# Split feed-forward weights: cut twice, or cut once, stored to DRAM and loaded again

## The chip, the cores and the metric

The kernel runs on one core of a Trainium2 chip. Its time is the device time of one execution in microseconds (us). The core has TensorE (PE, matrix products; its weight loads are shown apart as PEld), VectorE (DVE), ScalarE (ACT), GpSimd (POOL) and SyncE (SP), which here only issues DMAs. PEclk is the granted clock of TensorE as a share of full speed.

## What is computed

The reference chains two blocks over 2048 tokens of width 1024: a state-space and short convolution block, and then a block with a convolution module, a gated recurrence, chunked attention and a feed-forward part. Only the last part matters here, cut to its lines:

```
h = x * (1.0 + sc2) + sh2
gt, up = jnp.split(h @ w_ffn_in[l], 2, axis=-1)
y = (jax.nn.silu(gt) * up) @ w_ffn_out[l]
x = layer_norm(ALPHA * x + (1.0 + g2) * y, ln2_g[l], ln2_b[l])
```

All is float32. `w_ffn_in` is 1024 x 5632 (2816 gate columns, 2816 up columns), `w_ffn_out` 2816 x 1024. An operand of a product is scaled by a power of two and split into a high and a low f16 part; a product of two such operands is three f16 matmuls: high by high, high by low, low by high.

## The kernel before

The feed-forward part runs twice over the weights, once for each half of the tokens (1024). A half has two stages. The first makes the products with `w_ffn_in`, 256 columns at a time: a gate pair, then the up pair of the same columns, 11 of each, so 22 pairs for each half. The second makes the products with `w_ffn_out` and finishes rows (residual, layer norm); rows of the first half are finished while the second half's input products run.

The products of one pair use a scheme with 7 block products in place of 8 (`products`, L1967). Each block product is 4 slices of 128 by 3 f16 matmuls (lines L400, L401, L402), so 12 matmuls with 512 tokens; a pair has 84, a half 1848. Results leave PSUM by VectorE (L1979) and ScalarE (L1984).

A pair's weights (class `Pair`) go through three steps, in both halves alike:

- `load`: two DMAs of 512 KB (L1860) on SP's queue, into two raw float32 tiles.
- `scale`: two sums of squares on ScalarE (L393), their sum on VectorE (L1869), a reduction over all partitions on POOL (L361), a power of two from it on VectorE (L351 to L353).
- `cut`: four combinations of blocks on POOL (L357, 128x512 each), then four splits, each by one ScalarE instruction for the high part (L388) and one on VectorE for the low part (L389). The result is four f16 tiles of 7168 values per partition in all. Then the raw tiles are freed.

`Feed` decides when a pair's steps are issued: during the products of pair i (`ahead`, `later`) it issues the load, scale and cut of pair i+1 and the load and scale of pair i+2, as far as the arena (a planner of SBUF space) has room. A DMA that writes a raw tile waits until the cut of the pair that had the space before is done. SP issues its DMAs in the order in which they stand; one that waits holds up those behind it. All of the kernel's loads and stores named here stand in that one queue.

During the second half, SP also carries the loads and stores of the rows that are being finished (L2111 to L2135), which POOL and VectorE work on.

Of the kernel before, what the change touches and what calls it, by code (L numbers as in the profile page):

```python
# [10 lines left out]
F16 = mybir.dt.float16  # L11
# [9 lines left out]
P = 128  # L21
# [11 lines left out]
class Arena:  # L33
    def __init__(self, ap, n, unit, slack, small=0, zone=None):
        self.small = small
        self.zone = n if zone is None else zone
        self.ap = ap
        self.unit = unit
        self.slack = slack
        self.segs = [(0, n, 0)]  # L40
        self.now = 0
        self.live = {}
# [71 lines left out]
    def free(self, v):  # L114
        _, st, n, _ = self.live.pop(id(v))
        self.now += 1
        self.segs.append((st, st + n, self.now))
        self.segs.sort()
        old = self.now - self.slack
        out = []  # L120
        for s in self.segs:
            if out and out[-1][1] == s[0] and out[-1][2] <= old and s[2] <= old:
                out[-1] = (out[-1][0], s[1], max(out[-1][2], s[2]))
            else:
                out.append(s)
        self.segs = out
# [26 lines left out]
class Weight:  # L153
# [10 lines left out]
    def load(self):  # L164
        k = self.k
        self.raw = k.several([([P, self.nkb, P], F32, "raw")] * (self.ncol // P))
        for c, raw in enumerate(self.raw):
            k.nc.sync.dma_start(raw, self.src[:, c * P:(c + 1) * P].rearrange("(k p) c -> p k c", p=P))
# [101 lines left out]
class Kit:  # L270
# [69 lines left out]
    def keep(self, src):  # L340
        t = self.hold()
        self.nc.vector.tensor_copy(t, src)
        return t
# [755 lines left out]
def load_hT(k, dr_h, tb, t=None):  # L1099
    t = t or k.retry(lambda: k.pair([P, KB, TB], "hT"))  # L1100
    for x in range(2):
        k.nc.sync.dma_start(t[x].rearrange("p a b -> p (a b)"), dr_h[tb, x])
    return t
# [275 lines left out]
def stage_conv_att(k, ca, dr, hT, nxt):  # L1379
    att = None  # L1380
    for tb in range(NTB):
        if tb == 1:
            nxt()
        nh = None
        if tb + 1 < NTB:
            try:
                nh = k.pair([P, KB, TB], "hT") if AHEAD else None
            except MemoryError:
                pass
        if nh is not None:  # L1390
            load_hT(k, dr["h1"], tb + 1, nh)
        ca.proj(tb, hT)
        if nh is None and tb + 1 == NTB:
            nh = load_hT(k, dr["h1"], 0)
        k.free(*hT)
        hT = nh or load_hT(k, dr["h1"], tb + 1)
        if tb == 0:
            att = k.bg.add(ca.steps(), ATT_RATE)
            taps = k.bg.add(ca.taps(), EARLY_RATE)
    return att, taps, hT  # L1400
# [312 lines left out]
def stage_mix2(k, mx, dr, steps, taps, nxt):  # L1713
# [43 lines left out]
    def pairs(m):  # L1757
        he, ho = hs
        hs.clear()
        S, S_ = (k.new([P, 2, 512], F32, "S") for _ in range(2))  # L1760
        a11, a12, a21, a22 = he[:, :512], he[:, 512:], ho[:, :512], ho[:, 512:]
        k.gtt(S[:, 0], a21, a22, ALU.add)
        k.gtt(S[:, 1], S[:, 0], a11, ALU.subtract)
        k.gtt(S_[:, 0], a11, a21, ALU.subtract)
        k.gtt(S_[:, 1], a12, S[:, 1], ALU.subtract)
        later.append(lambda: cut(m, he, ho, a22, S, S_))
# [82 lines left out]
    return mv, k.rsqrt(mv[:, 1:2], 1.0, 1e-5)  # L1849


class Pair:
    def __init__(self, k, src, xinv):
        self.k, self.src, self.xinv = k, src, xinv

    def load(self):
        k = self.k
# [4 lines left out]
    def scale(self):  # L1862
        k = self.k
        ss = k.tiny("wss", 3)
        junk = k.new([P, 4, 2 * P], BF16, "junk")
        for i in range(2):
            k.sumsq(junk, self.raw[i], out=ss[:, i:i + 1])
        k.free(junk)
        k.nc.vector.tensor_tensor(ss[:, 2:3], ss[:, 0:1], ss[:, 1:2], ALU.add)  # L1869
        self.cols = k.cols3.pop(0) if len(k.cols3) > 8 else k.hold(3)  # L1870
        tot, self.s, self.inv = (self.cols[:, i:i + 1] for i in range(3))
        k.allsum(ss[:, 2:3], tot)
        k.pow2(tot, out=(self.s, self.inv))
        k.nc.vector.tensor_tensor(self.inv, self.inv, self.xinv, ALU.mult)

    def cut(self):
        k = self.k
        x, y = self.raw
        got = k.several([([P, 2, 4, 2 * P], F16, "w2")] * 2 + [([P, 2, 8, P], F16, "w3"), ([P, 2, 4, P], F16, "w1"), ([P, 8, P], F32, "T"), ([P, 4, P], F32, "T")])
        self.w, self.T = got[:4], got[4:]  # L1880
        b11, b12, b21, b22 = x[:, :, :P], x[:, :, P:], y[:, :, :P], y[:, :, P:]
        T, T4 = self.T
        T2, T3 = T[:, 0:4], T[:, 4:8]
        k.gtt(T3, b22, b12, ALU.subtract)
        k.gtt(b12, b12, b11, ALU.subtract)
        k.gtt(T2, b22, b12, ALU.subtract)
        k.gtt(T4, T2, b21, ALU.subtract)
        for i in (1, 0, 2, 3):
            t = self.w[i]
            k.split(t[:, 0], t[:, 1], (x, y, T, T4)[i], self.s)  # L1890
        k.free(*self.raw, *self.T)
        self.raw = self.T = None

    def block(self, b):
        t, o = ((self.w[0], 0), (self.w[1], 0), (self.w[1], P), (self.w[0], P), (self.w[2], 0), (self.w[2], 4), (self.w[3], 0))[b]
        if t.shape[3] == 2 * P:
            return [(t[:, 0, i, o:o + P], t[:, 1, i, o:o + P]) for i in range(4)]
        return [(t[:, 0, o + i], t[:, 1, o + i]) for i in range(4)]

    def free(self):  # L1900
        self.k.free(*self.w)
        self.k.cols3.append(self.cols)


class Feed:
# [30 lines left out]
class FFN:  # L1936
# [7 lines left out]
    def prep(self, inv_h, ln):  # L1944
        k, a = self.k, self.a
        self.ln = ln
        DFF = self.FB * P
        Wi = a["w_ffn_in_2"][0]
        self.chunks = [Feed([Pair(k, Wi[:, c + f * P:c + f * P + 2 * P], inv_h) for f in range(0, self.FB, 2) for c in (0, DFF)]) for _ in range(2)]

    def prime(self, hf):
        f = self.chunks[hf]
# [251 lines left out]
@with_exitstack  # L2204
def two_blocks(ctx, tc, a, out):
    k = Kit(ctx, tc)
    dp = ctx.enter_context(tc.tile_pool(name="dr", bufs=1, space=DRAM))
    dr = {
        "u": dp.tile([512, 8, 256], F32, name="u_d"),
        "y": dp.tile([512, 8, 256], F32, name="y_d"),  # L2210
        "yv": dp.tile([512, T], F32, name="yv_d"),
        "mod": dp.tile([1, 6 * D], F32, name="mod_d"),
        "x2": dp.tile([T, D], F32, name="x2_d"),
        "y2": dp.tile([T, D], F32, name="y2_d"),
        "x3": dp.tile([T, D], F32, name="x3_d"),
        "z": dp.tile([T, 512], F32, name="z_d"),
        "h1": dp.tile([NTB, 2, P, KB * TB], F16, name="h1_d"),
        "h2": dp.tile([4, 2, P, 28 * P], F16, name="h2_d"),
        "ext": dp.tile([4, P * 768 + 768], F32, name="ext_d"),
    }  # L2220
    xT, chunks, ssm, mod = stage_in(k, a, dr)
    ca = ConvAtt(k, a, dr)
    rec = Rec(k, a, dr)
    mx = Mix2(k, a, dr)
    ff = FFN(k, a, dr, out)
    tk = {}

    def start_c(tb, ih, hb):
        if tb == 1:
            tk["c"] = k.bg.add(ca.prep(ih, hb), 1.0)  # L2230
        if tb == 2:
            tk["hT"] = load_hT(k, dr["h1"], 0)

    inv_h, hb2 = stage_glu_mix(k, a, xT, chunks, ssm, mod, dr, start_c)
    k.bg.drain(tk["c"])

    def start_r():
        tk["r"] = k.bg.add(rec.prep(inv_h), 1.0)

    att, taps, hT = stage_conv_att(k, ca, dr, tk["hT"], start_r)  # L2240

    def start_m():
        tk["m"] = k.bg.add(mx.prep(), 0.4)

    steps = stage_rec(k, rec, dr, hT, att, taps, start_m)
    k.bg.drain(tk["m"])
    ff.prep(mx.inv_h, mx.ln)
    hT = stage_mix2(k, mx, dr, steps, taps, lambda t: ff.prime(0) if t >= PRIME_AT else None)
    ff.run(hT)
# [26 lines left out]
```

## Time and profile before

| | us |
|---|---|
| three runs | 3523.9, 3524.34, 3530.92 (median 3524.34) |
| profiled execution, span | 3526.9 |
| first half, input products | 2068 to 2536 |
| first half, output products | 2543 to 2777 |
| second half, input products | 2777 to 3280 |
| second half, output products | 3287 to 3510 |

The page gives the profiled execution's span and no other time of it, so sums are made against that span. The stages are read from the times of the matmuls by line. A row of groups shows: line, engine, operation, tiles written and read, count, busy time, mean ns, then the idle time of the engine before these instructions and what ended it. A row of windows shows for each engine its busy time in a stretch, the granted clock, the DMA engines' share and GB/s. A row of waits shows the engine and line, what released it, and then the total, the number and the longest.

### The profile page before, as it was taken

Reading aid. Unit: us, or ns where it says so; the run is one execution under the profiler, and the core shown is the slowest. Engines: PE = TensorE matmul, PEld = TensorE weight load, DVE = VectorE, ACT = ScalarE, POOL = GpSimd, SP = SyncE. Lnnn points to the kernel's source line nnn. Section 1 sums busy time; section 2 is a strip of 40 time slices with the busy share of each in tenths; the row PEclk is TensorE's granted clock in tenths of the full one; section 3 lists DMA queues with packets and bytes.
Section 4 is the critical chain, followed back from the end, with each engine's and each line's share of the span. In section 5 each row is a group of like instructions: output and inputs, shape, how many; then the busy total and the mean of one; then the engine's idle time right before and its main releaser. Section 6 shows DMA issues by size and latency. Waiting matters only on the chain. (4 is left out here: it accounts for less than half of the span.)

```text
span 3526.9 us, 44439 instructions
## 1 busy us (share of the span) xinstructions
PE 3094.7 (88%) x16116; PEld 1533.4 (43%) x16116; DVE 2270.6 (64%) x5218; ACT 1285.4 (36%) x1986; POOL 916.3 (26%) x1018
## 2 busy tenths in 40 slices
PE   5688999999689888999899968898799987997998
PEld 3244444534245554555554423343344432433444
DVE  5475877366655579997678776666523587655446
ACT  4322222574335564222243335554411233443210
POOL 0243335033332332010301233332101344321012
PEclk9889999999889999999999989999999998998999
DMA  8623534435475661100347972211414112111421
GB/s 181 145 74 86 134 89 105 109 102 161 140 237 108 120 140 37 37 33 16 105 132 166 242 203 90 96 54 46 139 58 144 62 63 79 45 48 48 152 90 51
DMA packets 534844, 367.79 MB, mean 104 GB/s; under 512 B 290952, under 2 KB 480328, under 8 KB 530528
## 3 DMA queue, kind: packets, MB, share of 16 engines
q1 hardware_dynamic: 534624, 364.95, 38.1%
q8 instruction: 126, 2.06, 0.2%
q14 instruction: 94, 0.77, 0.1%
HBM read 236.91 MB, written 67.66 MB: 86 GB/s over the span
## 5 line engine op out<-in xcount | busy, mean ns | idle before, releaser
L400 PE MATMUL psum<-arena 128*128 128x512 f16 (+2 forms) x4272 | 1617.1, 380 | 254.4 <-ACT arena L388 161.8
L402 PE MATMUL psum<-arena 128*128 128x512 f16 (+2 forms) x4272 | 1613.1, 379 | 33.5 <-DVE arena L389 30.1
L401 PE MATMUL psum<-arena 128*128 128x512 f16 (+2 forms) x4272 | 1616.0, 380 | 19.3 <-DMA arena<-h_d 15.4
L357 POOL TENSOR_TENSOR arena<-arena 128x64 f32<-128x64 f32 (+4 forms) x794 | 785.4, 1010 | 1617.8 <-issue 300.8
L400 PEld LDWEIGHTS <-arena 128*128 128x128 f16 x4272 | 428.4, 100 | 704.8 <-ACT arena L388 144.4
L389 DVE SCALAR_TENSOR_TENSOR arena<-arena,kept 128x1024 f16<-128x1024 f32 (+2 forms) x394 | 480.6, 1244 | 334.0 <-ACT arena L388 332.6
L388 ACT ACTIVATE arena<-arena,kept 128x1024 f16<-128x1024 f32 (+2 forms) x394 | 388.5, 1013 | 771.9 <-DVE kept L352 256.1
L402 PEld LDWEIGHTS <-arena 128*128 128x128 f16 x4272 | 427.0, 100 | 546.7 <-DVE arena L389 49.7
L401 PEld LDWEIGHTS <-arena 128*128 128x128 f16 x4272 | 427.0, 100 | 537.2 <-issue 100.4
L393 ACT ACTIVATE arena<-arena 128x1024 bf16<-128x1024 f32 (+2 forms) x262 | 284.0, 1084 | 492.2 <-DVE arena L2038 93.4
L361 POOL PARTITION_ALL_REDUCE kept<-ring x95 | 49.5, 529 | 614.0 <-issue 265.1
L1979 DVE TENSOR_TENSOR arena<-arena,psum 128x512 f32<-128x512 f32 x264 | 176.1, 679 | 24.1 <-PE psum L402 14.7
L351 DVE TENSOR_SCALAR ring<-kept 128x1 int32<-128x1 int32 x141 | 20.7, 151 | 249.0 <-POOL kept L361 217.4
L1350 DVE SCALAR_TENSOR_TENSOR arena<-arena 128x512 f32<-128x512 f32 x240 | 177.7, 775 | 0.3
L1532 PE MATMUL psum<-arena 128*127 128x64 f32 (+6 forms) x896 | 103.6, 260 | 21.5 <-DVE arena L1535 20.7
L1532 PEld LDWEIGHTS psum<-arena 128*127 128x127 f32 (+6 forms) x896 | 99.6, 178 | 47.8 <-DVE arena L1535 29.0
L389 DVE SCALAR_TENSOR_TENSOR arena<-arena,ring 128x1024 f16<-128x1024 f32 x76 | 103.6, 1374 | 21.2 <-ACT arena L388 21.2
L388 ACT ACTIVATE arena<-arena,ring 128x1024 f16<-128x1024 f32 x76 | 85.9, 1141 | 82.2 <-DVE ring L352 44.8
L753 DVE SCALAR_TENSOR_TENSOR arena<-arena 128x128 f32<-128x128 f32 x336 | 105.0, 349 | 1.6
L1270 ACT ACTIVATE arena<-arena,ring,kept 128x640 f32<-128x640 f32 (+4 forms) x64 | 54.4, 851 | 91.0 <-DVE ring L1268 74.7
L2038 DVE SCALAR_TENSOR_TENSOR arena<-arena,kept 128x512 f32<-128x512 f32 x88 | 78.9, 898 | 1.2
L1534 DVE TENSOR_TENSOR arena<-arena 128x256 f32<-128x256 f32 x112 | 55.7, 497 | 34.2 <-PE psum L1532 33.5
(315 smaller groups left out, 2662.5 us busy)
## 6 DMA issues: line engine op xcount, KB each, us to landing
arena<-in_w_ffn_in_dram SPq DMA_DIRECT2D x88, 512.0 KB
arena<-in_w_in_dram SPq DMA_DIRECT2D x50, 512.0 KB
arena<-in_w_ada_dram SPq DMA_DIRECT2D x48, 512.0 KB
arena<-h_d SPq DMA_DIRECT2D x22, 1024.0 KB
arena<-in_w_ffn_out_dram SPq DMA_DIRECT2D x88, 256.0 KB
arena<-in_x_dram SPq DMA_DIRECT2D x32, 512.0 KB
x_d<-arena SPq DMA_DIRECT2D x32, 512.0 KB
arena<-in_w_ffn_out_dram SPq DMA_DIRECT2D x22, 512.0 KB
```

What stands on the lines that cost most here:

```text
L357: self.nc.gpsimd.tensor_tensor(out, x, y, op)
L388: self.nc.scalar.activation(hi, src, AF.Identity, scale=s)
L389: self.nc.vector.scalar_tensor_tensor(lo, src, s, hi, op0=ALU.mult, op1=ALU.subtract)
L393: self.nc.scalar.activation(junk, src, AF.Square, accum_out=ss)
L400: self.nc.tensor.matmul(ps, lh, rh, start=start and i == 0, stop=False)
L401: self.nc.tensor.matmul(ps, lh, rl, start=False, stop=False)
L402: self.nc.tensor.matmul(ps, ll, rh, start=False, stop=stop and i == n - 1)
L753: v.scalar_tensor_tensor(ac, raw[:, kb], cc[:, kb:kb + 1], ac, op0=ALU.mult, op1=ALU.add)
L1350: v.scalar_tensor_tensor(acc[:, f], src, w, acc[:, f], op0=ALU.mult, op1=ALU.add)
L1532: nc.tensor.matmul(pv[:rows, bsl], KS[:, c * P:c * P + rows], q4[:, bsl], start=True, stop=True)
L1979: v.tensor_tensor(out, x, ps, op)
L2038: v.scalar_tensor_tensor(g[f][:, j], u, wu.inv, g[f][:, j], op0=ALU.mult, op1=ALU.mult)
```

## The change

In the first half, the last act of `cut` now is `keep`: the four f16 tiles of a pair are stored to a DRAM array `w2` (22 pairs, 128 partitions, 7168 values), by four DMAs on SP's queue, three of 512 KB and one of 256 KB, 1.835 MB for each pair, 88 DMAs in all. In the second half a new class `Again` takes the place of `Pair`: its `load` is four DMAs from that array straight into four f16 tiles; its `scale` and `cut` do nothing, and the inverse scale is the one that the first half kept. In place of two raw loads of 512 KB each, a pair of the second half has those four.

```
+PIECES = ((0, (2, 4, 2 * P)), (2048, (2, 4, 2 * P)), (4096, (2, 8, P)), (6144, (2, 4, P)))
...
-        self.cols = k.cols3.pop(0) if len(k.cols3) > 8 else k.hold(3)
-        tot, self.s, self.inv = (self.cols[:, i:i + 1] for i in range(3))
+        tot, self.s, self.inv = k.tiny("ptot"), k.tiny("ps"), k.hold()
...
         for i in (1, 0, 2, 3):
             t = self.w[i]
             k.split(t[:, 0], t[:, 1], (x, y, T, T4)[i], self.s)
+        self.keep()
         k.free(*self.raw, *self.T)
...
+    def keep(self):
+        for (o, shape), t in zip(PIECES, self.w):
+            n = shape[0] * shape[1] * shape[2]
+            self.k.nc.sync.dma_start(self.kept[:, o:o + n], t.rearrange("p x a b -> p (x a b)"))
...
     def free(self):
         self.k.free(*self.w)
-        self.k.cols3.append(self.cols)
...
+class Again(Pair):
+    def __init__(self, first):
+        self.k, self.first, self.kept = first.k, first, first.kept
+
+    def load(self):
+        k = self.k
+        self.inv = self.first.inv
+        self.w = k.several([([P, *shape], F16, "w%d" % i) for i, (_, shape) in enumerate(PIECES)])
+        for (o, shape), t in zip(PIECES, self.w):
+            n = shape[0] * shape[1] * shape[2]
+            k.nc.sync.dma_start(t.rearrange("p x a b -> p (x a b)"), self.kept[:, o:o + n])
+
+    def scale(self):
+        pass
+
+    def cut(self):
+        pass
...
-        self.chunks = [Feed([Pair(k, Wi[:, c + f * P:c + f * P + 2 * P], inv_h) for f in range(0, self.FB, 2) for c in (0, DFF)]) for _ in range(2)]
+        cols = [c + f * P for f in range(0, self.FB, 2) for c in (0, DFF)]
+        first = [Pair(k, Wi[:, c:c + 2 * P], inv_h, self.dr["w2"][i]) for i, c in enumerate(cols)]
+        self.chunks = [Feed(first), Feed([Again(w) for w in first])]
...
+        "w2": dp.tile([FFN.FB, P, 7168], F16, name="w2_d"),
```

Lines move by the change: the raw load L1860 becomes L1863, the store is L1900, the new load L1922, and later lines stand 28 further (L2073 becomes L2101). On SP's queue, the end of the first half's input products and the start of the output products before (`in_w_ffn_in` are raw loads of weights, `in_w_ffn_out` those of the output products, `h_d` activations):

```order
L1860 DMA arena<-in_w_ffn_in_dram 128x4x256 x4
L2018 DMA arena<-in_w_ffn_out_dram 128x1024 x2
L1860 DMA arena<-in_w_ffn_in_dram 128x4x256 x16
L2073 DMA arena<-in_w_ffn_out_dram 128x512 x7
L2169 DMA arena<-h_d 128x4x1024
```

and the end of the same stretch now (`w_d` is the array `w2`):

```order
L1863 DMA arena<-in_w_ffn_in_dram 128x4x256 x2
L1900 DMA w_d<-arena 128x2048 x3
L1900 DMA w_d<-arena 128x1024
L1863 DMA arena<-in_w_ffn_in_dram 128x4x256 x2
L1900 DMA w_d<-arena 128x2048 x3
L1863 DMA arena<-in_w_ffn_in_dram 128x4x256
L1900 DMA w_d<-arena 128x1024
L1863 DMA arena<-in_w_ffn_in_dram 128x4x256
L2101 DMA arena<-in_w_ffn_out_dram 128x512 x4
L1900 DMA w_d<-arena 128x2048 x3
L1900 DMA w_d<-arena 128x1024
L1922 DMA arena<-w_d 128x2048
```

Between the loads of one pair and the next, four stores of the pair that has just been cut now stand; the last two loads L1863 apart are those of pair 21.

In the second half ScalarE before had, for each pair, squares (the L393 rows) and four cuts (the three and one L388 rows) between the PSUM copies L1984 and the activations' own squares and cuts (those with `ring`):

```order
L388 ACTIVATE arena<-arena,ring 128x1024 x2
L1984 COPY arena<-psum 128x512
L388 ACTIVATE arena<-arena,kept 128x1024 x3
L388 ACTIVATE arena<-arena,kept 128x512
L393 ACTIVATE arena,ring<-arena 128x1024 x2
L2029 ACTIVATE arena<-arena,kept 128x1024 x2
L1984 COPY arena<-psum 128x512
```

and now has only the copy and the activations' work:

```order
L2012 COPY arena<-psum 128x512
L393 ACTIVATE arena,kept<-arena 128x1024
L388 ACTIVATE arena<-arena,ring 128x1024
L393 ACTIVATE arena,kept<-arena 128x1024
L2012 COPY arena<-psum 128x512
L388 ACTIVATE arena<-arena,ring 128x1024
```

The weights' squares (L393 into `ring`) and cuts (L388 with `kept`) are gone from between the copies; what stays belongs to the activations and, as L2029 before and L2057 now, to the gate.

More of the change, by code (lines that the diff above doesn't have):

```diff
@@ L1849, in ln_stats, with __init__ @@
     return mv, k.rsqrt(mv[:, 1:2], 1.0, 1e-5)
+PIECES = ((0, (2, 4, 2 * P)), (2048, (2, 4, 2 * P)), (4096, (2, 8, P)), (6144, (2, 4, P)))
 class Pair:
-    def __init__(self, k, src, xinv):
-        self.k, self.src, self.xinv = k, src, xinv
+    def __init__(self, k, src, xinv, kept):
+        self.k, self.src, self.xinv, self.kept = k, src, xinv, kept
     def load(self):
```

## The prediction

> **What bounds the kernel now.** I read the page's first line, then cut the span at the stages of the feed-forward part, and then read TensorE's waits in each of them.
>
> ```profile
> PE 3094.7 (88%) x16116; PEld 1533.4 (43%) x16116; DVE 2270.6 (64%) x5218; ACT 1285.4 (36%) x1986; POOL 916.3 (26%) x1018
> core 0: us, PE busy (x) PEld busy (x) DVE busy (x) ACT busy (x) POOL busy (x), PEclk, DMA share, GB/s
> 2068.00:2536.00 468.00, 401.86 (x1765) 173.78 (x1764) 290.47 (x476) 230.36 (x313) 132.71 (x104) 0.94 0.29 89
> 2543.00:2777.00 234.00, 231.53 (x1057) 104.01 (x1057) 74.01 (x111) 45.51 (x64) 26.05 (x21) 0.99 0.31 104
> 2777.00:3280.00 503.00, 421.96 (x1849) 182.03 (x1848) 332.90 (x571) 200.03 (x261) 174.43 (x137) 0.93 0.19 64
> ```
>
> TensorE is the bound of the whole, and the rows are, in order: the input products of the first half of the tokens (all but some 80 matmuls; the records lack a few), the output products of that half, and the input products of the second half. Output products keep TensorE busy for 231.53 of 234 us. Input products don't: 81 us are missing in the second half and 66 in the first. The waits of TensorE say for what; first the second half, then the first:
>
> ```profile
> PE psum L400 <- ACT arena L388: 66.6, 10, 15.7
> PE psum L402 <- DVE arena L389: 14.2, 15, 1.7
> ...
> PE psum L400 <- ACT arena L388: 40.4, 11, 7.5
> PE psum L402 <- DVE arena L389: 13.3, 15, 1.8
> ```
>
> L388 and L389 make the f16 high and low part of a weight tile, so TensorE waits for weights to be cut. The chain ahead of a cut is seen on late pairs 20 and 21 of the first half (SP's queue, then POOL, ScalarE, TensorE):
>
> ```profile
> 2466.33 0.37 SPq L1860 DMA_DIRECT2D arena<-in_w_ffn_in_dram  x1
> 2469.22 0.37 SPq L1860 DMA_DIRECT2D arena<-in_w_ffn_in_dram  x1
> 2487.97 0.37 SPq L1860 DMA_DIRECT2D arena<-in_w_ffn_in_dram  x1
> 2491.63 0.37 SPq L1860 DMA_DIRECT2D arena<-in_w_ffn_in_dram  x1
> ...
> 2473.01 3.98 POOL L357 TENSOR_TENSOR arena<-arena 128x512 f32<-128x512 f32 x3 [3.82 <-DMA arena<-in_w_ffn_in_dram]
> 2482.82 0.40 POOL L361 PARTITION_ALL_REDUCE kept<-ring  x1 [5.83 <-issue]
> 2490.33 1.27 POOL L357 TENSOR_TENSOR arena<-arena 128x512 f32<-128x512 f32 x1 [7.10 <-issue]
> ...
> 2483.64 3.23 ACT L388 ACTIVATE arena<-arena,kept 128x1024 f16<-128x1024 f32 x3 [6.05 <-DVE kept L352]
> 2511.98 3.23 ACT L388 ACTIVATE arena<-arena,kept 128x1024 f16<-128x1024 f32 x3 [5.67 <-DVE kept L352]
> ...
> 2485.88 0.39 PE L400 MATMUL psum<-arena 128*128 128x512 f16 x1 [1.68 <-ACT arena L388]
> 2514.22 0.61 PE L400 MATMUL psum<-arena 128*128 128x512 f16 x1 [6.72 <-ACT arena L388]
> ```
>
> One raw buffer pair is left there, so the loads of pair 21 start only when pair 20 is cut (2487.97, 2491.63), land some 3.8 us later, and sums, all-reduce and cuts follow. TensorE starts pair 20 at 2485.88 and pair 21 at 2514.22, each as soon as its first cut is there.
>
> **Second half: what goes.** All of that chain is removed there for 22 pairs: 4 combinations and an all-reduce on POOL, 2 squares and 4 cuts on ScalarE, 4 cuts on VectorE and small scale work. In the groups of that stage:
>
> ```profile
> L357 POOL TENSOR_TENSOR arena<-arena 128x512 f32<-128x512 f32 x118 | 166.6, 1425 | 203.9 <-issue 78.8 <-DMA arena<-in_w_ffn_in_dram 59.1 <-ACT arena L393 15.2
> L361 POOL PARTITION_ALL_REDUCE kept<-ring x19 | 7.8, 414 | 112.1 <-issue 85.8 <-DVE arena L2113 13.8 <-DVE ring L1869 6.7
> L389 DVE SCALAR_TENSOR_TENSOR arena<-arena,kept 128x1024 f16<-128x1024 f32 x60 | 81.4, 1384 | 16.8 <-ACT arena L388 16.5
> L389 DVE SCALAR_TENSOR_TENSOR arena<-arena,kept 128x512 f16<-128x512 f32 x20 | 17.2, 859 | 18.5 <-ACT arena L388 18.5
> ```
>
> About 19 to 20 pairs are cut inside this stage (2 or 3 were primed during the output products, where TensorE is full). What is left for VectorE is at most 332.90 - 81.4 - 17.2 = 234 us, and less for ScalarE and POOL: none can bound a stage of 400 us.
>
> What TensorE gives then follows from its spacing, running free and just after a long stall:
>
> ```profile
> 2481.66 0.38 PE L401 MATMUL psum<-arena 128*128 128x512 f16 x1
> 2483.82 0.38 PE L402 MATMUL psum<-arena 128*128 128x512 f16 x1
> ...
> 2882.56 0.61 PE L400 MATMUL psum<-arena 128*128 128x512 f16 x1 [13.64 <-ACT arena L388]
> 2885.70 0.63 PE L400 MATMUL psum<-arena 128*128 128x512 f16 x1
> 2887.84 0.63 PE L402 MATMUL psum<-arena 128*128 128x512 f16 x1
> ```
>
> Between the first two rows lie 10 matmuls, so 2.16/10 = 0.216 us each; between the last two 5, so 2.14/5 = 0.428, half the rate. A pair is 84 matmuls (7 products of 12), 22 pairs are 1848, and at 0.2157 (the spacing with one more digit, over longer stretches) that is 398.6 us; at the mean of the output products (231.53/1057 = 0.219) it is 405. The stage takes 503. Its loss of 104 is 66.6 + 14.2 = 80.8 of stalls, and 503 - 80.8 - 398.6 = 23 of slow matmuls behind stalls, which go with them. [...]
>
> I keep 5 us for what remains (the rows' other waits, and the 405 above), from 1 to 15: the second half gains **99 us** (90 to 104).
>
> **Second half: what comes.** Four loads for each pair, 1.835 MB in place of 1.05 MB, 88 in all, on SP. At TensorE's pace of 18.1 us (84 x 0.2157) they need 1.835/18.1 = 101 GB/s. What the same queue moved in its best and in a common stretch:
>
> ```profile
> 2680.00:2690.00 10.00, 10.00 (x48) 4.54 (x47) 3.52 (x5) 1.15 (x2) 1.26 (x1) 1.00 0.89 282
> 1990.00:2000.00 10.00, 10.00 (x48) 4.54 (x47) 7.82 (x21) 4.60 (x5) 2.89 (x3) 1.00 1.03 211
> ```
>
> So 6.5 to 8.7 us of 18.1. The loads write their tiles as soon as an earlier pair's products have read them; by the order of waits that is at least 140 matmuls, or 30 us, before TensorE reads them. They share SP with the rows of the first half that are being finished:
>
> ```profile
> SPq L2135 <- POOL arena L357: 102.1, 16, 29.5
> ```
>
> Here SP waits for POOL up to 29.5 us, with loads behind it. POOL's long delays come from the weight work that leaves, so I cost this at 0, and at 1 to 3 waits of 15 us if it stays: 0 to 45 us, kept as a rival below.
>
> **First half: what is added.** 88 stores, 1.835 MB for each pair, 3 pieces of 512 KB and one of 256 KB, each behind its cut, in SP's queue. An issue takes 0.37 us of SP. For a late pair, three stores now stand ahead of the next pair's first load and a fourth ahead of its second. These loads are on the chain. The issue costs at least 3 x 0.37 = 1.1 us for the first load and 1.5 for the second; beyond it, up to 1.57 MB are begun ahead of the load's bytes, 5.6 us at 282 GB/s and 7.4 at 211, if nothing of it had drained. But the pieces are cut at least 3.23/3 = 1.1 us apart (row 2483.64), and a piece of 0.52 MB needs 1.9 us at 282: I estimate that about half has drained when the load is issued. So 1.1 to 7.4 us, and I take 3.5 for the pair. Two things point up: the second load decides when POOL starts (row 2473.01), and it stands behind the most. From the trace, the chain passes a delay to TensorE in full: in the late pairs TensorE waits at each start.
>
> How many pairs? Pairs 18 to 21 have a single raw buffer, so the load waits for the cut: 4 x 3.5 = 14 us. In the pairs before, a second raw buffer lets a load go ahead of the cut, by the order; I take 2 us for all of them. One early place is worse, where the weights of pair 3 are loaded:
>
> ```profile
> 2109.85 1.37 SPq L1860 DMA_DIRECT2D arena<-in_w_ffn_in_dram  x2
> 2115.99 6.18 POOL L357 TENSOR_TENSOR arena<-arena 128x512 f32<-128x512 f32 x4 [13.73 <-DMA arena<-in_w_ffn_in_dram]
> 2131.80 0.61 PE L400 MATMUL psum<-arena 128*128 128x512 f16 x1 [5.54 <-ACT arena L388]
> ```
>
> POOL had been idle for 13.73 us when those bytes came, and TensorE stood for 5.54 at the pair's start. Pair 2's four stores now precede this load: 1.79 MB, 6.3 us at 282 and 8.5 at 211, against 1.5 of issue alone. I take 7. Sum: 14 + 2 + 7 = **23 us** lost, from 8 (4 x 1.1 + 1.5 + 2) to 40 (4 x 7.4 + 8.5 + 2).
>
> [...]
>
> **Sum.** The profiled execution spans 3526.9 us, 2.6 above the median of 3524.34. 3526.9 - 99 + 23 = 3451; against the median 3524.3 - 76 = **3448 us**. Its own range, by the bounds, is 3524.3 - 104 + 8 = 3428 to 3524.3 - 90 + 40 = 3474.
>
> **The rivals.**
>
> *Stores cost nothing* in the first half: stores drain while ScalarE still cuts, and only the second half's 99 count: 3425. For it speaks that the first half moves 89 GB/s of 282 seen; against it the four late loads that wait for the very cuts that the stores follow.
>
> *More of the first half pays.* If the stores cost 4 us on each of the last 11 pairs, not 4, the loss is 44 + 7 = 51, so 3524 - 99 + 51 = 3476. For it: 11 waits of TensorE on L388 in that half, so most late pairs have no slack. Against: their loads were issued earlier.
>
> *The loads of the second half become the bound.* At the 89 GB/s of the first half as a whole, 1.835 MB take 20.6 us, 22 pairs 453 us: 50 gained, 23 lost, 3497. The same comes of three waits of SP on POOL of 15 us. Against: 282 GB/s seen, 30 us of lead.
>
> *Slower.* In the first half SP's queue becomes the bound: each store waits for its cut, and every next pair's load waits behind it for all of the 1.57 MB. At 5.6 us for each of 22 pairs that is 123 - 99 = 24 us more than before: 3548. It decides from 99/22 = 4.5 us a pair. For it: a load behind a store that waits for a cut can't be early any more. Against: early pairs have a spare raw buffer, and the order leaves loads ahead of stores there.
>
> *It doesn't do what it says*: TensorE could wait in the second half for activations instead (L388's other work, or the sums that empty PSUM), which the weight work now hides. VectorE's 234 us in 400 speak against it; 30 us of it would give 3478, inside the range.
>
> **How the numbers follow.** Forecast 0.58 (3448); stores free 0.13 (3425); more of the first half 0.16 (3476); loads or activations bound the second half 0.07 (3490); slower 0.06 (3548). The likeliest case's own range is 3428 to 3474; the range 8 times in 10 is 3426 to 3488. A measurement of this kernel tells 0.2%, 7 us, from no change. Faster 0.92, same 0.02, slower 0.06.
>
> **What would show it.** In the profile after, the second half's input products should take 398 to 410 us, with TensorE's waits on cut weights gone and PEclk near 0.99; a wait on the new loads there means the third rival. In the first half the stage should take 490, not 468; waits for L388 should grow in the last four pairs and at pair 3. If that stage grows by under 8, the stores are free; by over 40, more pairs pay. The output products should stay at 234 and 223 us. Wrong it is if SP's waits hold back loads in either half by more than the cover named.

## The result, and the profile after

The changed kernel takes 3444.64 us (median of 4 runs, 3438.11 to 3448.44) beside 3526.59 of the kernel before on the same occasion: a ratio of 0.977, with a 95% interval of 0.9755 to 0.9784, 82 us faster. Measured again later beside other kernels it took 3445.32 where the kernel before took 3534.07: 0.9749 (0.9735 to 0.9762), 89 us faster. The forecast was 3448, 76 faster, in a range of 3426 to 3488.

The windows of the changed kernel's stages, and below them its waits of TensorE in the first half's input products (the second half's list of waits is empty; the 16.5 us, in pair 1, stand in place of 11.6 there and 5.8 at the start of pair 2 before):

```profile
core 0: us, PE busy (x) PEld busy (x) DVE busy (x) ACT busy (x) POOL busy (x), PEclk, DMA share, GB/s
2068.00:2548.00 480.00, 408.37 (x1766) 175.42 (x1765) 289.54 (x476) 231.84 (x315) 134.01 (x104) 0.93 0.49 167
2555.00:2785.00 230.00, 229.85 (x1056) 103.56 (x1056) 61.92 (x88) 30.18 (x44) 12.92 (x10) 0.99 0.35 120
2785.00:3184.00 399.00, 399.00 (x1850) 180.72 (x1849) 204.37 (x393) 81.51 (x104) 49.61 (x38) 1.00 0.35 113
3195.00:3426.00 231.00, 230.73 (x1056) 103.74 (x1055) 113.22 (x211) 29.42 (x44) 29.85 (x22) 0.99 0.24 85
```

```profile
PE psum L400 <- ACT arena L388: 47.6, 13, 7.0
PE psum L400 <- ACT arena L2012: 16.5, 1, 16.5
PE psum L402 <- DVE arena L389: 7.3, 8, 1.8
```

In the second half TensorE now never stops: 399.00 us busy of 399.00, clock 1.00, all 22 pairs 18.1 us long. That is the floor worked out beforehand. In the first half the stage grew. To see where, the pairs were counted off in the matmul records, 84 matmuls to a pair. Lengths in us, each from one profiled execution; the rows below the change are the experiments that follow:

| | pairs 0-1 | pairs 2-9 | pairs 10-16 | pairs 17-21 | first half | second half |
|---|---|---|---|---|---|---|
| before | 73.5 | 179.4 | 136.8 | 113.2 | 502.9 | 502.8 |
| the change | 72.6 | 182.4 | 136.5 | 123.7 | 515.3 | 398.9 |
| the change, again | 71.0 | 184.9 | 138.3 | 123.9 | 518.1 | 398.9 |
| stores only | 71.2 | 185.6 | 138.7 | 124.9 | 520.4 | 505.5 |
| small stores | 72.2 | 176.5 | 136.0 | 116.0 | 500.7 | 506.4 |
| scale once, no stores | 71.6 | 175.7 | 135.9 | 113.8 | 496.9 | 425.9 |
| stores at low priority | 71.7 | 180.3 | 142.7 | 115.0 | 509.7 | 398.9 |
| pairs 5-10 stored | 72.8 | 178.4 | 137.7 | 113.0 | 501.9 | 407.0 |
| double loads | 72.9 | 184.9 | 138.8 | 125.1 | 521.7 | 398.9 |
| stores from ScalarE | 68.6 | 176.5 | 143.0 | 120.7 | 508.8 | 398.9 |
| pairs 5-16 stored | 71.8 | 177.3 | 136.2 | 115.5 | 500.8 | 407.5 |
| pairs 17-21 stored | 72.1 | 178.8 | 134.7 | 123.0 | 508.7 | 427.9 |

The profiled span is 3436.4, 90.5 below before: 103.9 gained in the second half's input products, 3.9 in the first half's output products (234.0 to 230.1), 12.4 lost in the first half's input products, 3.4 lost in the gap ahead of the last stage, 1.5 lost in that stage (229.7 to 231.2: before, its last matmul ends at 3517.0, behind the 3510 of the table of stages, so the prediction's 223 is 7 us short). This profiled run was the fastest of the four; in the profile of the second measurement (3444.3) the first half lost 15.2.

The late pairs lose most, and unevenly. Counted from the start of the pair before, pairs 18 and 19 start 5.8 and 5.7 us later than they did, pair 20 1.8 later, and pair 21 2.7 sooner. The chain for pair 19, before and then in the changed kernel: SP's queue, then POOL, then TensorE at the start of pair 19.

```profile
2443.66 1.52 SPq L1860 DMA_DIRECT2D arena<-in_w_ffn_in_dram  x2
2449.66 4.30 POOL L357 TENSOR_TENSOR arena<-arena 128x512 f32<-128x512 f32 x3 [8.95 <-DMA arena<-in_w_ffn_in_dram]
2464.10 0.39 PE L400 MATMUL psum<-arena 128*128 128x512 f16 x1 [1.38 <-ACT arena L388]
```

```profile
2451.50 3.37 SPq L1900 DMA_DIRECT2D w_d<-arena  x4
2454.98 1.52 SPq L1863 DMA_DIRECT2D arena<-in_w_ffn_in_dram  x2
2461.20 7.05 POOL L357 TENSOR_TENSOR arena<-arena 128x512 f32<-128x512 f32 x4 [13.14 <-DMA arena<-in_w_ffn_in_dram]
2477.71 0.61 PE L400 MATMUL psum<-arena 128*128 128x512 f16 x1 [5.05 <-ACT arena L388]
```

Pair 18 starts at 2443.37 before and at 2451.25 now. The second load of pair 19 went out 1.4 us behind that start (2444.81) and now goes 4.6 behind it (2455.89), after four stores that each wait for their own cut. So 3.2 of the 5.7 us are the later issue. Another 0.5 is the longer way from issue to POOL, 2.6 stand between POOL's start and the reduction, which now has four combinations ahead of it and not three, and 0.6 comes back behind it.

The same for pair 20 of the changed kernel:

```profile
2477.96 3.45 SPq L1900 DMA_DIRECT2D w_d<-arena  x4
2481.52 2.21 SPq L1863 DMA_DIRECT2D arena<-in_w_ffn_in_dram  x2
...
2488.84 4.29 POOL L357 TENSOR_TENSOR arena<-arena 128x512 f32<-128x512 f32 x3 [14.26 <-DMA arena<-in_w_ffn_in_dram]
...
2501.26 0.39 PE L400 MATMUL psum<-arena 128*128 128x512 f16 x1 [1.71 <-ACT arena L388]
```

Both loads of pair 20 now go out within 2.21 us, behind four stores; before, the first went 2.9 us ahead of the second (2466.33 and 2469.22). POOL starts 6.2 us after the second issue (2482.66), where it was 3.8 (2469.22 to 2473.01). TensorE starts pair 20 18.6 us after that issue, where it was 16.7. Here the issue is no later against the start of pair 19 (4.95 us behind it, 5.12 before).

The early pairs lose elsewhere than foretold. Pair 3 waits about as long as before (5.07 us, 5.54 before). Pair 4 waits 3.85 us at its start, where it was 1.01, and TensorE stands again inside pair 4, four products in. TensorE's rows, SP's waits from 2140 to 2170, and ScalarE's square that waits for the load:

```profile
2128.43 0.61 PE L400 MATMUL psum<-arena 128*128 128x512 f16 x1 [5.07 <-ACT arena L388]
...
2152.75 0.39 PE L400 MATMUL psum<-arena 128*128 128x512 f16 x1 [3.85 <-ACT arena L388]
...
2169.25 0.39 PE L400 MATMUL psum<-arena 128*128 128x512 f16 x1 [4.28 <-ACT arena L388]
```

```profile
SPq L1900 <- DVE ring L351: 7.3, 1, 7.3
SPq L1900 <- DVE arena L389: 6.5, 1, 6.5
SPq L1863 <- DVE kept L1876: 6.2, 1, 6.2
...
2165.75 1.06 ACT L393 ACTIVATE arena<-arena 128x1024 bf16<-128x1024 f32 x1 [4.34 <-DMA arena<-in_w_ffn_in_dram]
```

SP stands 7.3 and 6.5 us with stores that wait, raw loads queued behind them, then 6.2 us with a raw load that waits itself, and ScalarE then stands 4.34 us for such a load. SP's standing alone doesn't make the loss: in the kernel before it stood 19.3 us with one raw load between 2140 and 2175. Pair 4 takes 28.6 us in place of 19.0. Part comes back: pairs 6 to 8 are 7.0 us shorter together than before, and pair 9, which has a long wait in both kernels, starts 2.7 us later than before, not 8.5 as pair 5 does.

### The profile page after: what moved, and what is told of

Same layout as the page of the kernel before. It is cut to its first block, busy times and chain, and to the rows that moved or that the text cites. A ratio compares the mean times of both kernels' runs of the same rounds, so it can differ in the third digit from the quotient of the medians.

```text
span 3436.4 us, 44077 instructions
## 1 busy us (share of the span) xinstructions
PE 3075.3 (89%) x16116; PEld 1532.4 (45%) x16116; DVE 2131.4 (62%) x5020; ACT 1152.9 (34%) x1810; POOL 779.6 (23%) x908
## 5 line engine op out<-in xcount | busy, mean ns | idle before, releaser
L357 POOL TENSOR_TENSOR arena<-arena 128x64 f32<-128x64 f32 (+6 forms) x706 | 656.4, 953 | 1544.9 <-issue 237.9
L402 PEld LDWEIGHTS <-arena 128*128 128x128 f16 x4272 | 425.9, 100 | 512.3 <-issue 37.6
L389 DVE SCALAR_TENSOR_TENSOR arena<-arena,kept 128x1024 f16<-128x1024 f32 (+2 forms) x218 | 260.3, 1212 | 255.5 <-ACT arena L388 255.0
L393 ACT ACTIVATE arena<-arena 128x1024 bf16<-128x1024 f32 (+2 forms) x218 | 237.7, 1091 | 520.6 <-DVE arena L2066 145.7
L388 ACT ACTIVATE arena<-arena,kept 128x1024 f16<-128x1024 f32 (+2 forms) x218 | 212.2, 995 | 497.7 <-PE psum L402 224.8
L389 DVE SCALAR_TENSOR_TENSOR arena<-arena,ring 128x1024 f16<-128x1024 f32 (+1 forms) x164 | 213.8, 1325 | 78.4 <-ACT arena L388 78.1
L388 ACT ACTIVATE arena<-arena,ring 128x1024 f16<-128x1024 f32 (+1 forms) x164 | 174.2, 1085 | 200.6 <-DVE ring L352 109.4
L361 POOL PARTITION_ALL_REDUCE ring<-ring x32 | 15.2, 478 | 478.9 <-DMA arena<-in_ln_b_dram 263.0
L361 POOL PARTITION_ALL_REDUCE kept<-ring x51 | 30.3, 603 | 354.6 <-issue 122.2
L2057 ACT ACTIVATE arena<-arena,kept 128x1024 f32<-128x1024 f32 x44 | 49.6, 1142 | 158.6 <-DVE arena L2007 158.5
```

The source lines that it names most:

```text
L357: self.nc.gpsimd.tensor_tensor(out, x, y, op)
L388: self.nc.scalar.activation(hi, src, AF.Identity, scale=s)
L389: self.nc.vector.scalar_tensor_tensor(lo, src, s, hi, op0=ALU.mult, op1=ALU.subtract)
L393: self.nc.scalar.activation(junk, src, AF.Square, accum_out=ss)
L402: self.nc.tensor.matmul(ps, ll, rh, start=False, stop=stop and i == n - 1)
```

## The experiments

**Stores only.** The second half is as before; what is stored is never read.

```
-        self.keep()
+        if self.kept is not None:
+            self.keep()
...
-        self.chunks = [Feed(first), Feed([Again(w) for w in first])]
+        self.chunks = [Feed(first), Feed([Pair(k, Wi[:, c:c + 2 * P], inv_h, None) for c in cols])]
```

> The first half stores all cut weights as the change does; the second half loads raw weights and cuts them again as before (what is stored is never read). By my theory (the second half's gain is the missing chain; the first half pays for the stores) the first half's input products take 513 to 517 us (503 before, 515 with the change), the second half's 500 to 506, and the time is 7 to 14 us above before. A rival, that the first half's 12 us come from the order that the planner chose around the new loads and not from the stores, expects no more than 3 us above before.

It measured 3555.45 beside 3533.61: 1.0063 (1.0047 to 1.0078), 22 us slower, of an interval of 17 to 28. Its last five pairs of the first half, and its second half:

```profile
2435.60:2560.54 124.94, 101.96 (x420) 42.20 (x421) 65.88 (x106) 43.91 (x57) 27.01 (x21) 0.89 0.37 128
2799.11:3304.59 505.48, 423.90 (x1849) 182.60 (x1848) 331.89 (x571) 199.47 (x260) 173.06 (x137) 0.92 0.20 63
```

The late pairs take 124.9 as in the change, the second half the time of before. So the loss of the first half is the stores' own, and storing alone gains nothing. The size was missed: the expectation, drawn from the profile of the change's fastest run, said 7 to 14, and 513 to 517 for the stage, which took 520.4. The 22 of these runs and the 104 of the second half make 82, the first measurement of the change. By stages the sum is less clean. The first half's input products take 17.5 us longer here than before; 8 more of the profile's 25 us lie ahead of their first matmul, which starts anywhere from 2028.2 to 2040.2 in the profiles of this document, with stores or without.

**Small stores.** As above, but each store writes 128 values per partition.

```
-            self.k.nc.sync.dma_start(self.kept[:, o:o + n], t.rearrange("p x a b -> p (x a b)"))
+            self.k.nc.sync.dma_start(self.kept[:, o:o + P], t.rearrange("p x a b -> p (x a b)")[:, :P])
```

> As the run with stores alone, but each of the 88 stores writes 128 of its 2048 or 1024 values per partition (32 KB in place of 512 or 256 KB), so a 15th of the bytes with the same number of issues and the same waits for cuts. If the bytes ahead of the loads cost the time (theory), the first half's input products take 503 to 507 us and the time is 0 to 4 us above before. If it is the issues, and the waits for cuts in SP's queue (rival), they take 512 to 517 and the time is 7 to 14 us above before.

3533.16 beside 3533.61: 0.9998 (0.9985 to 1.001). The late pairs:

```profile
2419.55:2535.54 115.99, 98.44 (x420) 41.91 (x421) 63.99 (x105) 45.21 (x58) 24.89 (x22) 0.93 0.24 69
```

Of the 11.7 us that five late pairs lost with full stores (124.9 against 113.2), 2.8 stay with a fourteenth of the bytes and the same 20 issues; kernels that store nothing there take 113.0 to 115.5, so this is little more than their scatter. Three or four stores still go out in the 8 us ahead of each late pair's second load, so issues alone cost little. The bytes are not the only difference, though: here the first load of pair 19 goes out between the stores of pair 18, and the second 2.2 us after pair 18's start, where the change has both behind all four stores and the second at 4.6. The early pairs lose nothing either (176.5), although SP still stands with stores, here from 2140 to 2175:

```profile
SPq L1901 <- ACT arena L388: 27.4, 7, 16.5
```

The planner orders the early stores and loads otherwise in this kernel, so what makes the early loss (bytes, waits in the queue, or that order) isn't told apart by it, and for the late pairs bytes and order changed together too.

**Scale once.** Nothing is stored; the second half loads raw weights and cuts them, with the first half's scale.

```
+class Redo(Pair):
...
+    def scale(self):
+        self.s, self.inv = self.first.s, self.first.inv
...
-        self.chunks = [Feed(first), Feed([Again(w) for w in first])]
+        self.chunks = [Feed(first), Feed([Redo(w) for w in first])]
```

> Nothing is stored. The second half loads raw weights and cuts them again as before, but takes the scale from the first half: no squares, no reduction over partitions, no power of two there. The four combinations on POOL and the eight split instructions stay. Theory (the second half's loss is the length of a serial chain behind one raw buffer): without about 10 us of squares, reduction and the idle time around it, the chain takes 12 to 16 us a pair, under TensorE's 18.1, so the second half's input products take 399 to 420 us, the first half's 503, and the time is 80 to 103 us below before. Rival (POOL's, ScalarE's and VectorE's work on cuts as such holds TensorE up): 450 us or more, and at most 50 us below before.

3456.74 beside 3533.61: 0.9785 (0.977 to 0.9801), 77 us faster, 3 less than the least expected. This keeps, in the second half, the four combinations and eight split instructions of each pair, and yet three quarters of the stage's gain are there. Its second half, and its longest wait there:

```profile
2775.92:3201.85 425.93, 404.21 (x1849) 181.46 (x1848) 319.20 (x475) 158.80 (x184) 184.26 (x118) 0.97 0.23 74
...
2918.60 0.61 PE L400 MATMUL psum<-arena 128*128 128x512 f16 x1 [14.72 <-ACT arena L388]
```

POOL has as much to do as before (184 us against 174), VectorE nearly so (319 against 333); ScalarE is spared the squares (159 against 200, of 503 us). It was not the work of cutting as such that held TensorE up in the kernel before, but the length of a chain in which squares, reduction and scale came between load and cut. The stage is 6 us longer than expected. What is left lies in three pairs (33.9, 23.1 and 24.5 us for pairs 6, 7 and 9, and 18.1 for each other). SP's queue there, from 2860 to 3000, says what holds up the raw loads:

```profile
SPq L2171 <- POOL arena L357: 48.6, 8, 13.4
```

L2171 in this kernel stores finished rows of the first half; SP stands up to 13.4 us with them while POOL works on those rows; 30.7 of the 48.6 us lie in the 35 us up to the end of TensorE's longest wait.

**Stores at low priority.** The change, with stores that the planner puts behind whatever else can go.

```
-        self.keep()
+        with self.k.rush(-100000):
+            self.keep()
```

> The change, with its stores put at the lowest priority of the planner: between two late pairs one store of 512 KB stands ahead of the next pair's first load on SP's queue in place of three or four, and the others behind the loads. Theory (bytes ahead of the loads): the first half's input products take 504 to 510 us in place of 515, the second half's 399, and the time is 86 to 93 us below before. Rival (stores cost the same wherever they stand, since they share the DMA engines): 513 to 517 us, and 78 to 84 below before.

3435.54 beside 3533.61: 0.9724 (0.9706 to 0.9742), 98 us faster, more than expected. The late pairs, with the same bytes stored (144 GB/s against 134 in the change):

```profile
2422.84:2537.86 115.02, 98.09 (x420) 41.68 (x421) 63.91 (x105) 45.27 (x58) 24.80 (x22) 0.93 0.42 144
```

115.0, not 123.7: here the stores cost most where they stand ahead of a load that is on the chain. With stores behind it the load is still used 0.5 to 1.2 us later after its issue than in the kernel before, 3.7 us over pairs 18 to 21. In the middle pairs this order loses 6 us (142.7); why was not followed up.

**The change again.**

> The change itself once more, beside the next three kernels on one chip. By the sums so far: the second half's input products 399 us, the first half's 513 to 522, the time 76 to 88 us below before. Were the first measurement an accident of the chip, it would lie outside.

3445.32 beside 3534.07, 89 us faster, 1 more than the expectation allowed. The first half took 518.1, the second 398.9.

**Some pairs stored.** Pairs 5 to 10 stored at low priority, the others cut again with the first half's scale.

```
-first = [Pair(k, Wi[:, c:c + 2 * P], inv_h, self.dr["w2"][i]) for i, c in enumerate(cols)]
+first = [Pair(k, Wi[:, c:c + 2 * P], inv_h, self.dr["w2"][i] if 5 <= i <= 10 else None) for i, c in enumerate(cols)]
-        self.chunks = [Feed(first), Feed([Again(w) for w in first])]
+        self.chunks = [Feed(first), Feed([Redo(w) if w.kept is None else Again(w) for w in first])]
```

> Pairs 5 to 10 of the first half are stored (at the planner's lowest priority) and loaded ready-made in the second; the 16 others are loaded raw and cut again there, with the first half's scale. In the run with the scale taken once, all lost time of the second half lay at pairs 6 to 9, while rows were being finished. Theory (the raw pairs lose only where SP and POOL serve those rows, and stores cost only where the next load waits for a cut): second half 399 to 406 us, first half 500 to 508, and the time 95 to 108 us below before. Rival (raw pairs elsewhere lose too, once the rows are finished sooner or later): second half 415 to 430, 70 to 90 below before.

3435.29 beside 3534.07: 0.9724 (0.9702 to 0.9747), 99 us faster. The first half took 501.9, as without stores. The second took 407.0, 1 more than expected. Its wait:

```profile
PE psum L400 <- DVE arena L2018: 5.8, 4, 2.7
```

That is TensorE waiting for VectorE to empty PSUM (L2018 is the addition that was L1979), not for weights. No wait on weights is left.

**Double loads.** Each ready-made tile of the second half is loaded twice.

```
+        for (o, shape), t in zip(PIECES, self.w):
+            n = shape[0] * shape[1] * shape[2]
+            k.nc.sync.dma_start(t.rearrange("p x a b -> p (x a b)"), self.kept[:, o:o + n])
```

> The change, with each ready-made tile of the second half loaded twice over (the second load of a tile waits for the first): 3.67 MB for each pair in 18.1 us, 203 GB/s. Theory (the loads have 30 us of lead, and 211 to 282 GB/s were seen): the second half stays at 399 to 405 us and the time within 8 us of the change. Rival (the loads were near the bound): 1.835 MB more for each pair at 211 GB/s or less leaves the second half at 420 us or more, with waits of TensorE on the loads.

3448.15, where the change took 3445.32 beside it. The second half:

```profile
2795.07:3193.93 398.86, 398.86 (x1849) 180.80 (x1848) 202.17 (x395) 81.28 (x104) 49.17 (x38) 1.00 0.61 197
```

197 GB/s in place of 113, and TensorE doesn't notice. Twice these loads still fit under their cover.

**Stores from ScalarE's queue**, at low priority.

```
-            self.k.nc.sync.dma_start(self.kept[:, o:o + n], ...)
+            self.k.nc.scalar.dma_start(self.kept[:, o:o + n], ...)
```

> The change, with its stores issued from ScalarE's queue at the lowest priority, so that no store stands ahead of a load in SP's order. Theory (the place in SP's queue is what costs): first half 503 to 510 us, the time 85 to 95 us below before. Rival (ScalarE, which makes the cuts, now waits for VectorE's low parts and issues 88 DMAs): 515 us or more, and 60 to 80 below before.

3438.0 beside 3534.07: 0.9732 (0.9719 to 0.9746), 96 us faster, 1 more than expected. The first half is 508.8 as expected, but the late pairs are no theory's:

```profile
2427.19:2547.86 120.67, 102.64 (x420) 42.71 (x421) 62.53 (x106) 44.06 (x57) 23.99 (x21) 0.88 0.39 137
```

120.7 lies between the 115.0 of low priority on SP and the 123.7 of the change, although no store stands ahead of a load in SP's order. The trace says where: the second loads of pairs 18 to 21 go out at most 0.6 us later than before (that of pair 21 4.3 sooner), but POOL, which waits for them, starts 6.0 to 9.1 us after their issue, where it was 3.6 to 4.9. So here the loads are later with stores under way from the other queue, and not by their place in SP's order; that it is the stores' bytes that delay them is the author's reading, not tested by itself.

**Where the stores stand.** Two kernels with scale once; stores at normal priority behind their cuts, in the first for pairs 5 to 16, in the second for pairs 17 to 21 alone.

```
-... self.dr["w2"][i] if 5 <= i <= 10 else None ...
+... self.dr["w2"][i] if 5 <= i <= 16 else None ...
```

> Only pairs 5 to 16 of the first half are stored, at normal priority, right behind their cuts as in the change, and loaded ready-made; the ten others are cut again in the second half with the first half's scale. Theory (the change's stores cost at the last five pairs and the first five, where the next load waits on SP's queue, and 0 to 2 us between, where a second raw buffer lets loads go ahead): first half 501 to 507 us, of it 113 to 115 from the start of pair 17 to the end, second half 399 to 403, time 98 to 108 us below before. Rival (any store behind a cut costs its 0.5 to 0.9 us a pair, wherever it stands): first half 508 to 514, 90 to 97 below before.

> The opposite: only pairs 17 to 21 are stored and loaded ready-made, the 17 others are cut again in the second half with the first half's scale. Theory: from the start of pair 17 to the end of the first half's input products 122 to 126 us in place of 113, as with all stores, the stretch before it as in the kernel before; the second half as in the run with the scale taken once, 420 to 428 us; time 62 to 74 us below before. Rival (late pairs pay since earlier stores still fill the DMA queues): 113 to 117 us there, and 75 to 82 below before.

Pairs 5 to 16: 3437.52 beside 3529.71, 0.973 (0.9707 to 0.9754), 92 us faster; first half 500.8, second 407.5 with 6.7 us of the same waits on PSUM as above, which the expectation hadn't counted on. The expected 98 to 108 was missed; 92 lies where the rival had it, but the rival's 508 to 514 for the first half does not hold. (That profile is of the fastest of four runs, 14 us below the median.) Pairs 17 to 21: 3463.35, 0.9809 (0.9791 to 0.9826), 66 faster, as expected. The late pairs of the one, then of the other:

```profile
2413.93:2529.39 115.46, 98.18 (x420) 41.66 (x421) 64.88 (x106) 44.15 (x57) 25.57 (x21) 0.93 0.21 64
```

```profile
2425.16:2548.19 123.03, 100.41 (x420) 41.84 (x421) 65.46 (x105) 45.10 (x58) 27.48 (x22) 0.90 0.39 135
```

Twelve pairs stored in the middle cost nothing that the profile shows (500.8 against 496.9 and 502.9 without stores). Five late ones cost 10, alone as with all others. So it is the place in the chain: with one raw buffer, the next load waits for the same cuts that the stores follow. In the first of these kernels, by their order on the queue, the second loads of pairs 5 to 15 go out 28 to 53 us ahead of the pair's first matmul, those of pairs 16 to 21 only 17 to 23.

The traces also divide the late cost. For each of pairs 18 to 21, the time from the start of the pair before is cut at the issue of the pair's second raw load and at POOL's start, which waits for that load. The four pairs together, in us beside the kernel before, each from one profile:

| | to the load's issue | from issue to use | from use to the pair's start | sum |
|---|---|---|---|---|
| the change | 9.5 | 4.7 | -3.8 | 10.5 |
| the change, again | 11.0 | 3.7 | -3.2 | 11.6 |
| stores only | 11.5 | 3.8 | -3.7 | 11.7 |
| pairs 17-21 stored | 8.3 | 5.3 | -3.3 | 10.4 |
| small stores | 3.4 | 0.0 | -0.3 | 3.0 |
| stores at low priority | 0.5 | 3.7 | -1.7 | 2.5 |
| stores from ScalarE | -3.3 | 13.2 | -1.8 | 8.1 |
| pairs 5-16 stored (none of these) | 1.6 | 0.4 | 0.6 | 2.7 |

With stores ahead of it the load goes out 8 to 12 us later over the four pairs and is used 4 to 5 us later after its issue; with stores behind it, at low priority, it goes out only 0.5 us later, and the 3.7 us from issue to use stay. The last row shows how far a kernel strays that stores nothing there.

Of all these, four versions come out about as fast as one another and faster than the change by their medians: stores at low priority (0.9724), pairs 5 to 10 stored (0.9724), pairs 5 to 16 stored (0.973), stores from ScalarE's queue (0.9732). Their intervals lie below the first measurement of the change (0.977) and overlap those of the second (0.9749) a little, so the gain over the change, 3 to 10 us beside the second measurement, is seen in the first half's stage rather than proved by the times.

## Why the prediction was right

**The second half's gain** was foreseen as 99, from 90 to 104, and is 104. The floor of 398.6 was right to 0.3 us. The 5 us kept for remaining waits were not needed: without the weight work VectorE is 204 us busy (234 were set as the upper bound) and TensorE finds everything ready. The 23 us of slow matmuls (0.428 us each behind a wait of 13.64 us, 0.216 running free) went with the stalls, as argued: PEclk is 1.00 there, where it was 0.93, with no idle time and 18.1 us for each of 22 pairs. Which stalls slow the matmuls behind them, and for how long, was not tested.

**The cause was right in kind, and sharper than told.** The prediction spoke of weights to be cut and of a chain behind one raw buffer. Scale once shows that it is the chain's length: cutting again costs the second half 27 us, squares, reduction and scale the other 77.

**The loads of the second half** were costed at 0, and cost 0; double loads keep it. Of the rival that finished rows hold them up, the trace shows SP's waits for POOL down from 102.1 to 52.1 us (16 waits, the longest 7.8), as POOL's weight work left:

```profile
SPq L2163 <- POOL arena L357: 52.1, 16, 7.8
```

**The first half's loss** was foreseen as 23, from 8 to 40. By whole times the stores alone cost 22, but the stage itself lost less: 12.4 and 15.2 with the change, 17.5 with the stores alone. This term was too large and the gain of 99 too small, which is why 76 was forecast and 82 to 89 measured. Its terms are less exact than their sum. Pairs 18 to 21 at 3.5 each, 14, measured 10 to 12 (from the start of pair 17 to the end), but as 5.8, 5.7, 1.8 and -2.7: that four equal terms come near the sum is partly luck. The 2 us for the middle are 0 to 2. The 7 us of pair 3 were put in the wrong place: that pair lost nothing, and 3 to 6 us beside the profile before (which with the kernels without early stores spreads from 175.7 to 179.4) are lost over pairs 2 to 9, mainly inside pair 4, where stores and loads wait in turn on SP's queue; what of that sets the loss stays open.

**What delays a late load** was put as 1.1 to 1.5 us of issues and, for the rest, bytes begun ahead of it, half drained by the author's estimate. That is the smaller part. In the change the load goes out 9.5 us later over the four pairs, behind stores that wait for their own cuts, and is used 4.7 us later after its issue. The wait behind stores stands in the prediction only under the rival "slower", and three stores ahead of the first load fit pair 21 alone: for pair 20 the order shown has all four ahead of both loads, and pair 19's rows have the same. Pair 20's second load went from 3.8 to 6.2 us between issue and use, 2.4 more, less than the 5.6 that 1.57 MB would add at 282 GB/s if all of it went ahead of the load and none had drained by its issue; whether stores had drained, or moved beside the load, was not shown.

**Not foreseen** was the gap ahead of the last stage, which grew from 7.4 to 10.8 us. The changed kernel there, VectorE and TensorE:

```profile
3184.06 0.69 DVE L2179 TENSOR_SCALAR arena<-arena 128x1024 f32<-128x1024 f32 x1 [1.70 <-DMA arena<-in_ln_g_dram]
3189.47 0.69 DVE L2178 TENSOR_SCALAR arena<-arena 128x1024 f32<-128x1024 f32 x1 [1.85 <-DMA arena<-mod_d]
...
3195.07 0.59 PE L400 MATMUL psum<-arena 128*128 128x512 f16 x1 [10.84 <-ACT arena L388]
```

VectorE stands 1.70 and 1.85 us there for rows of the last layer norm, with the last activations' sums and scales behind them. Together that is 3.55; in the profile before, such waits of 1.64 and 0.75 stand there, so only 1.2 of the 3.4 can be put down to them. It was not tested. The ready-made loads are not needed for it: scale once, which has none, shows a gap of 10.0. Four us came back in the first half's output products (234.0 to 230.1), where the first pairs of the second half are no longer cut: POOL is busy there for 12.92 us in place of 26.05, ScalarE for 30.18 in place of 45.51. That is not the reason, or not alone, for with stores only, which cuts those pairs as before, the stage takes as little:

```profile
2568.23:2799.11 230.88, 230.13 (x1056) 103.71 (x1056) 74.12 (x111) 45.42 (x64) 26.07 (x21) 0.99 0.32 106
```

**The rivals.** Stores free (3425) holds for the middle pairs only. More of the first half paying (3476) fell: the seven pairs 10 to 16 lose 0 to 2 us together. Loads as the bound (3497) and slower (3548) fell, as TensorE has no wait on the new loads, nor on activations in the change's second half, and stores alone cost 22, not 123.

## What to carry to other kernels

Before paying memory traffic to avoid work done twice, look which part of that work lies on the chain: here keeping 22 scales, with no weights stored, gave 77 us, where storing all the weights gave 82 to 89. Where results were stored for later here, it counted less how many bytes went out than which load stood behind them: the same 1.835 MB a pair cost nothing that was seen where a second buffer let the next load go ahead (pairs 5 to 16 stored, 500.8 us beside 496.9 and 502.9 without stores), and about 2 us a pair where the load waited for the same cuts (pairs 17 to 21). For the late pairs the shared queue did best with the loads on the chain first (115.0 us, 123.7 in the change); a queue of their own for the stores took the wait away, but the loads were used 6.0 to 9.1 us after their issue, where it was 3.6 to 4.9 (120.7 us).

## What the runs showed of the hardware

TensorE ran 1849 matmuls over 398.86 us without one gap while the DMAs moved 197 GB/s on average, with a granted clock of 1.00: that much traffic cost it nothing in this stage, which took 398.87 us at 113 GB/s. And 88 more DMA issues on a queue, with few bytes (32 KB each), cost nothing measurable in 3533 us (0.9998, 0.9985 to 1.001). A raw load of 512 KB for pairs 18 to 21 was used 3.6 to 4.9 us after its issue in the kernel before, and 6.0 to 9.1 us after it with stores under way from ScalarE's queue.
